# Second layer's modulation weights in rings of their own, loaded two steps ahead, in a two-layer transformer kernel on one NeuronCore

## The chip, the cores and the metric

The kernel runs on 1 core of one Trainium2 chip. The metric is the device time of one execution in microseconds (us). The engines are TensorE (PE for matmuls, PEld for its weight loads), VectorE (DVE), ScalarE (ACT), GpSimd (POOL) and SyncE (SP, which here issues the transfers, DMAs, one after another). TensorE's granted clock is shown as a share of 2.4 GHz; 0.50 is 1.2 GHz.

## The reference

For a sequence of 512 rows of width 1024, each of two layers computes

```python
mod = jnp.einsum('bd,lde->lbe', jax.nn.silu(c), ada_w) + ada_b[:, None]
for i in range(DEPTH):                               # DEPTH = 2
    sh_t, sc_t, g_t, sh_c, sc_c, g_c = [m[:, None] for m in jnp.split(mod[i], 6, axis=-1)]
    h = x * (1.0 + sc_t) + sh_t
    y = mixer_i(h)                                   # layer 0: sparse attention; layer 1: differential attention
    x = _layer_norm(DN_ALPHA * x + (1.0 + g_t) * y, ln_g[i, 0], ln_b[i, 0])
    h = x * (1.0 + sc_c) + sh_c
    y = jnp.square(jax.nn.relu(h @ mlp_w1[i])) @ mlp_w2[i]      # 1024 -> 4096 -> 1024
    x = _layer_norm(DN_ALPHA * x + (1.0 + g_c) * y, ln_g[i, 1], ln_b[i, 1])
```

All is float32. The change concerns `mod` of layer 1: one vector of 1024 times a matrix of 1024 x 6144 (24 MB), which is read from HBM once.

## The kernel before, in words

**Number format.** A float32 product is made of three TensorE passes on rounded parts: each operand x is split into a high part H (a rounded copy, by ACT) and a low part L = x - H (by DVE or POOL). `mm3` and the `step` of `out_proj` issue low x high, high x high, high x low. So each weight piece of 512 KB goes through four places: the load into a tile of ring `raw` (L128, SP; **3 buffers**), the cast to `wh` (L148, ACT), the subtraction to `wl` (L153, POOL and DVE in turn), and the matmuls. `wh` and `wl` have 6 buffers each.

**The MLP** (`mlp`, once for each layer) goes through the hidden width in four quarters q = 0 to 3. In each, the w1 product makes 8 tiles of 128 hidden units x 512 rows (24 matmuls a tile; lines L158 to L160), each followed by `act`: Relu on ACT (L1035), squared on DVE (L1037, tile `ex`, from a PSUM bank into SBUF), split into two pages (L133, L134). Then the w2 product of the quarter, `out_proj` (L549 to L551), has two halves h0 and h1 of 512 output columns: four row tiles i, 8 steps k, 3 matmuls, so 96 matmuls a half. A finished half is evicted by `add_scaled`: four products with the gain on DVE (L459, tile `pt`) and four additions to the residual R on POOL (L460). Banks: six PSUM banks in rings `psd`, `psl`, `pso` of two serve w1 tiles and w2 halves in turn, so a half of w2 can start in a bank only when what was in it has been evicted.

**Side work.** While layer 0's MLP (MLP 0) runs, the generator `side` makes layer 1's modulation: `ada_dve` loads 128 x 1024 weights (512 KB) into ring `raw`, and DVE adds them, scaled by silu(c), to accumulators `vo`: two instructions of 128 x 512 for each load (L429 for the first row block, L431 for the later ones). There are 3 pairs of vectors x 8 row blocks x 2 = 48 such steps. After each pair TensorE sums over the partitions (L436, matmuls with ones), and a copy, transposes and small additions (L439, L405, L415) give the columns `modc`. A `next(side)` stands behind every `act` and every k step of w2 in q = 1 to 3, and three in q = 0. In the same way `affine_later` (L534, L535, POOL) scales and shifts the residual R by the layer norm's pages, 8 steps, one behind each of the first acts of q = 0.

**Order.** The text's order is not the program's: a scheduler with a timeline of its own places the instructions of each engine, and each engine then runs its list in order. A `with tc.issue_after(ins)` keeps DVE instructions of the block behind `ins`; the loads on SP and the matmuls are not bound by it. Waits for data and for free buffers are semaphores. A load waits on SP for its ring's buffer, and every later load on SP waits behind it.

Of the kernel before, what the change touches and what calls it, by code (L numbers as in the profile page):

```python
# [15 lines left out]
ALU = mybir.AluOpType  # L16
# [3 lines left out]
P = 128  # L20
S = 512
D = 1024
DC = D // P
# [44 lines left out]
def hybrid_kernel(  # L68
# [8 lines left out]
    nc = tc.nc  # L77
    x = x[0]
    out = out[0]
# [4 lines left out]
    pg = ctx.enter_context(tc.tile_pool(name="pages", bufs=1))  # L84
# [12 lines left out]
    def page(dt=F32, tag="pg"):  # L97
        return pg.tile([P, 512], dt, tag=tag, name=nm(tag), bufs=GB[tag])
# [3 lines left out]
    def temp(tag, dt=F32):  # L102
        return tp.tile([P, 512], dt, tag=tag, name=nm(tag), bufs=TB[tag])
# [20 lines left out]
    def raw(shape, src, bufs=3):  # L124
        n = shape[0] * shape[1]
        t = wp.tile([P, 1024], F32, tag="raw", name=nm("raw"), bufs=bufs)
        v = t[:, :n].rearrange("p (a b) -> p a b", a=shape[0])
        nc.sync.dma_start(v, src)  # L128
        return v
# [79 lines left out]
    sil = cp.tile([P, 8], F32, name="sil")  # L209
# [29 lines left out]
    adaw = [ada_w[l].rearrange("(k p) n -> p k n", p=P) for l in range(2)]  # L239
# [60 lines left out]
    for kc in range(DC):  # L300
# [9 lines left out]
        a = (hT[0][:, kc, :], hT[1][:, kc, :])  # L310
# [91 lines left out]
    def ada_cols(l, va, vb, res, o, rows=P):  # L402
        ov = o.rearrange("p (m r) -> p m r", m=4)
        for m in range(4):
            nc.tensor.transpose(ov[:, m, 0:rows], res[0:rows, P * m : P * (m + 1)], ident[0:rows, 0:rows])  # L405
        for j in range(rows // 32):
            col = ov[:, :, 32 * j : 32 * j + 1].rearrange("p m o -> p (m o)")
            if vb is not None:
                v, h, partial = (va, vb)[j // 2], j % 2, False
            elif rows < P:  # L410
                v, h, partial = va, j, False
            else:
                v, h, partial = va, j // 2, j % 2 == 1
            c = slice(4 * h, 4 * h + 4)
            nc.vector.tensor_tensor(out=modc[:, l, v, c], in0=col, in1=modc[:, l, v, c] if partial else abcv(l, v)[:, c],  # L415
                                    op=ALU.add)

    def ada_dve(l, va, vb, tag):

        vs = (va,) if vb is None else (va, vb)  # L420
        acc = [page(tag=tag) for _ in range(4 if vb is not None else 2)]
        for k in range(DC):
            for n, v in enumerate(vs):
                r = raw((1, 1024), adaw[l][:, k : k + 1, D * v : D * (v + 1)])
                for h in range(2):
                    src = r[:, 0, 512 * h : 512 * (h + 1)]
                    a = acc[2 * n + h] if vb is not None else acc[h]
                    if k == 0:
                        nc.vector.tensor_scalar(out=a, in0=src, scalar1=sil[:, k : k + 1], scalar2=None, op0=ALU.mult)  # L429
                    else:  # L430
                        nc.vector.scalar_tensor_tensor(out=a, in0=src, scalar=sil[:, k : k + 1], in1=a,  # L431
                                                       op0=ALU.mult, op1=ALU.add)
                yield
        o = bank("t")
        for j in range(4 if vb is not None else 2):
            nc.tensor.matmul(o[32 * j : 32 * j + 32, :], ones[:, 0:32], acc[j], start=True, stop=True,  # L436
                             tile_position=(0, 32 * j))
        n = 128 if vb is not None else 64
        nc.vector.tensor_copy(acc[0][0:n], o[0:n])  # L439
        ada_cols(l, va, vb, acc[0], o, n)  # L440

    def gain(l, v, tag="pg"):

# [148 lines left out]
    def attend(pairs, make, mask, pv, done, out, LA, early=None, depth=1, group=0, side=iter(()),  # L592
# [117 lines left out]
        for _ in ahead:  # L710
# [7 lines left out]
                            op0=ALU.mult)  # L718
# [55 lines left out]
    for i in range(1, NT):  # L774
        W = P * (i + 1)
        acc = page()
        work[i] = acc
        for h in range(IDXH):
# [4 lines left out]
            r = temp("neg")  # L783
# [4 lines left out]
            else:  # L788
                nc.vector.scalar_tensor_tensor(out=acc[:, 0:W], in0=r[:, 0:W], scalar=s, in1=acc[:, 0:W],
                                               op0=ALU.mult, op1=ALU.add)  # L790
# [5 lines left out]
    for i in range(NT):  # L796
        if i % 2 == 0:
            ckb.append(bank("t"))
        o = ckb[-1][:, 256 * (i % 2) : 256 * (i % 2) + 256]
# [195 lines left out]
        return weights(), first, rest  # L995

    def next_mod():
        yield from ada_dve(0, 5, None, "pg")
        n = 0
        for va, vb in ((0, 1), (3, 4), (2, 5)):  # L1000
            for _ in ada_dve(1, va, vb, "vo"):
                n += 1
                if n % 6:
                    yield

    side = next_mod()
    R = [[None, None] for _ in range(NT)]
# [17 lines left out]
    def mlp(l, hT, ln_idx, coef_fn, side):  # L1025
        w1 = mlp_w1[l].rearrange("(k p) n -> p k n", p=P)
        w2 = mlp_w2[l].rearrange("(k p) n -> p k n", p=P)
        nT = []
        aff = affine_later()
        for q in range(4):  # L1030
            aT = []

            def act(o):
                r = temp("neg")
                nc.scalar.activation(r, o, AF.Relu)  # L1035
                a = temp("ex")
                nc.vector.scalar_tensor_tensor(out=a, in0=o, scalar=0.0, in1=r, op0=ALU.max, op1=ALU.mult)  # L1037
                H, L = page(F32R), page(F32R)
                split_sb(a, H, L, nc.vector)
                aT.append((H, L))  # L1040
                next(aff, None)
                if q:
                    next(side, None)

            ws, os = [], []
            for n in range(8):
                c0 = 1024 * q + P * n
                w = wpiece((8, P), w1[:, :, c0 : c0 + P])
                o = wide_bank()
                if q == 0 and n < 4:  # L1050
                    ws.append(w)
                    os.append(o)
                    denseT(o, w, hT, ((0, 256),))
                    if n == 3:
                        for m in range(4):
                            denseT(os[m], ws[m], hT, ((256, 512),))
                            act(os[m])
                else:
                    denseT(o, w, hT)
                    act(o)  # L1060
            if q == 0:
                for _ in aff:
                    pass
                for _ in range(3 if l == 0 else 0):
                    next(side, None)
                gc = gain(l, 5, "vo")
            fin = None
            if q == 3:
                coef = coef_fn() if coef_fn else None
                ln = ln_idx if coef else ln_pages(*ln_idx, "vo")  # L1070

                def fin(i):
                    if coef is not None and not nT:
                        nT.extend(new_hT())
                    finish(R[i], i, ln, coef, nT)

            wo = out_proj(w2[:, 8 * q : 8 * q + 8, :], lambda k: aT[k], 8, (0, 1, 2, 3), (None,) * 4,
                          (None, nc.vector if q == 3 else None))
            for k in range(8):
                next(wo)  # L1080
                if q:
                    next(side, None)
            run_out(wo, R, gc, fin)
        return nT

# [144 lines left out]
```

## Time and profile before

| what | value |
|---|---|
| median of 3 runs | 1328.95 us (1327.79 to 1335.72) |
| the profiled execution | 1328.26 us, its span 1326.5 us |
| PE busy in the span | 1263.0 us, 95% |
| DVE, ACT, POOL busy | 759.9, 503.0, 572.4 us |
| TensorE's granted clock, mean | 0.986 |
| MLP 0 | about 325 to 690 us |
| MLP 1 | about 968 to 1320 us |

"Waits" list, for an engine and a line, the time the engine stood idle just before that line's instructions and the instruction or transfer that ended the wait. A "timeline" lists instructions in order of time, with the idle time before each in brackets. "Windows" cut the span into stretches. L-numbers are lines of the kernel before; behind the change they are some 26 to 30 higher.

### The profile page before, as it was taken

Reading aid. Unit: us, or ns where it says so; the run is one execution under the profiler, and the core shown is the slowest. Engines: PE = TensorE matmul, PEld = TensorE weight load, DVE = VectorE, ACT = ScalarE, POOL = GpSimd, SP = SyncE. Lnnn points to the kernel's source line nnn. Section 1 sums busy time; section 2 is a strip of 40 time slices with the busy share of each in tenths; the row PEclk is TensorE's granted clock in tenths of the full one; section 3 lists DMA queues with packets and bytes.
Section 4 is the critical chain, followed back from the end, with each engine's and each line's share of the span. In section 5 each row is a group of like instructions: output and inputs, shape, how many; then the busy total and the mean of one; then the engine's idle time right before and its main releaser. Section 6 shows DMA issues by size and latency. Waiting matters only on the chain.

```text
span 1326.5 us, 17997 instructions
## 1 busy us (share of the span) xinstructions
PE 1263.0 (95%) x6546; PEld 1018.1 (77%) x6546; DVE 759.9 (57%) x1561; ACT 503.0 (38%) x969; POOL 572.4 (43%) x469
## 2 busy tenths in 40 slices
PE   7999998998998999979999999999899999999997
PEld 4775666677986878857788888877698888888885
DVE  2488769869644655666647276675764242241437
ACT  2454157724431222322424555673353142231320
POOL 1614358506383404505434774451548524424403
PEclk9999999999998999989999999999999999999998
DMA  9828577443525456656522533440044333333311
GB/s 290 222 86 251 147 201 206 123 144 103 176 80 175 159 174 193 188 174 206 159 80 80 159 96 91 137 119 13 23 137 152 100 97 96 96 96 95 95 48 64
DMA packets 170417, 176.82 MB, mean 133 GB/s; under 512 B 12796, under 2 KB 128856, under 8 KB 170328
## 3 DMA queue, kind: packets, MB, share of 16 engines
q1 hardware_dynamic: 170328, 175.67, 45.0%
q8 instruction: 52, 0.85, 0.3%
q14 instruction: 37, 0.30, 0.1%
HBM read 160.93 MB, written 2.12 MB: 123 GB/s over the span
## 4 chain that ended last, share of the span: by engine, by line
PE 51%; DVE 11%; DMA 10%; POOL 4%; issue 2%; ACT 2%; SPq 0%; DVEq 0%; POOLq 0%; ACTq 0%
DMA raw<-in_ada_w_dram 8%; PE psd L158 4%; PE psd L159 4%; PE psd L160 4%; DVE vo L431 2%; DMA raw<-in_mlp_w_dram 2%; PE psl L158 2%; PE psl L159 2%; PE psl L160 2%; PE pso L549 2%; PE pso L551 2%; PE pso L550 2%; PE psl L551 2%; PE psl L550 2%; PE psl L549 2%
## 5 line engine op out<-in xcount | busy, mean ns | idle before, releaser
L153 POOL TENSOR_TENSOR wl<-raw,wh 128x512 fp32r<-128x512 f32 (+1 forms) x226 | 300.8, 1356 | 501.1 <-ACT wh L148 499.3
L148 ACT CAST wh<-raw 128x1024 fp32r<-128x1024 f32 x181 | 189.6, 1049 | 405.2 <-DMA raw<-in_mlp_w_dram 130.7
L153 DVE TENSOR_TENSOR wl<-raw,wh 128x1024 fp32r<-128x1024 f32 x68 | 96.6, 1421 | 121.9 <-ACT wh L148 121.8
L158 PE MATMUL psd<-htl,wh 128*128 128x512 f32 (+1 forms) x400 | 156.8, 392 | 5.0 <-DVE htl L134 4.2
L159 PE MATMUL psd<-hth,wh 128*128 128x512 f32 (+1 forms) x400 | 154.1, 385 | 0.0
L160 PE MATMUL psd<-hth,wl 128*128 128x512 f32 (+1 forms) x400 | 153.6, 384 | 0.0
L460 POOL TENSOR_TENSOR rq<-rq,pt 128x512 f32<-128x512 f32 x66 | 97.9, 1513 | 93.1 <-DVE pt L459 93.0
L431 DVE SCALAR_TENSOR_TENSOR vo<-raw,sil,vo 128x512 f32<-128x512 f32 x84 | 78.7, 976 | 85.9 <-DMA raw<-in_ada_w_dram 85.9
L158 PEld LDWEIGHTS psd<-htl,wh 128*128 128x128 f32 x400 | 76.0, 190 | 27.2 <-DVE htl L134 5.3
L650 ACT ACTIVATE ex<-neg,mx 128x128 f32<-128x128 f32 (+3 forms) x128 | 72.1, 564 | 51.0 <-DVE mx L644 44.8
L134 DVE TENSOR_TENSOR pg<-ex,pg 128x512 fp32r<-128x512 f32 x66 | 66.8, 1013 | 39.4 <-ACT pg L133 39.4
L160 PEld LDWEIGHTS psd<-hth,wl 128*128 128x128 f32 x400 | 75.9, 190 | 15.0 <-POOL bm L637 0.8
L158 PE MATMUL psl<-htl,wh 128*128 128x512 f32 (+1 forms) x224 | 82.1, 366 | 4.2 <-DVE htl L134 4.2
L159 PEld LDWEIGHTS psd<-hth,wh 128*128 128x128 f32 x400 | 76.1, 190 | 12.7
L133 ACT CAST pg<-ex 128x512 fp32r<-128x512 f32 x66 | 40.9, 621 | 117.2 <-DVE ex L1037 116.2
L159 PE MATMUL psl<-hth,wh 128*128 128x512 f32 (+1 forms) x224 | 81.7, 365 | 0.0
L160 PE MATMUL psl<-hth,wl 128*128 128x512 f32 (+1 forms) x224 | 81.3, 364 | 0.0
L549 PE MATMUL psl<-wh,pg 128*128 128x512 f32 x176 | 69.8, 397 | 6.4 <-DVE pt L459 4.8
L549 PE MATMUL pso<-wh,pg 128*128 128x512 f32 x176 | 69.4, 394 | 2.6 <-DVE pt L459 2.6
L549 PE MATMUL psd<-wh,pg 128*128 128x512 f32 x160 | 63.0, 394 | 8.5 <-DVE ex L1037 8.5
L551 PE MATMUL psl<-wh,pg 128*128 128x512 f32 x176 | 69.6, 396 | 0.0
L550 PE MATMUL psl<-wl,pg 128*128 128x512 f32 x176 | 69.5, 395 | 0.0
(309 smaller groups left out, 2952.1 us busy)
## 6 DMA issues: line engine op xcount, KB each, us to landing
raw<-in_mlp_w_dram SPq DMA_DIRECT2D x128, 512.0 KB, 4.1
raw<-in_ada_w_dram SPq DMA_DIRECT2D x80, 512.0 KB, 4.3
raw<-in_b_w_in_dram SPq DMA_DIRECT2D x24, 512.0 KB, 3.8
pg<-pg SPq DMA_DIRECT2D x84, 128.0 KB, 2.5
pg<-in_ada_w_dram SPq DMA_DIRECT2D x32, 256.0 KB, 5.3
raw<-in_a_w_in_dram SPq DMA_DIRECT2D x14, 512.0 KB, 5.1
hk<-tbd SPq DMA_DIRECT2D x16, 256.0 KB, 4.0
raw<-in_a_w_o_dram SPq DMA_DIRECT2D x8, 512.0 KB, 5.4
```

Source lines behind the costliest of these rows:

```text
L134: eng.tensor_tensor(out=L, in0=src, in1=f(H), op=ALU.subtract)
L148: nc.scalar.copy(Hv, r)
L153: eng.tensor_tensor(out=Lv[:, a:b], in0=r[:, a:b], in1=f(Hv[:, a:b]), op=ALU.subtract)
L158: nc.tensor.matmul(o, w[0], a[1], start=first, stop=False)
L159: nc.tensor.matmul(o, w[0], a[0], start=False, stop=False)
L160: nc.tensor.matmul(o, w[1], a[0], start=False, stop=last)
L431: nc.vector.scalar_tensor_tensor(out=a, in0=src, scalar=sil[:, k : k + 1], in1=a, op0=ALU.mult, op1=ALU.add)
L460: eng.tensor_tensor(out=R[h], in0=R[h], in1=t, op=ALU.add)
L549: nc.tensor.matmul(o, al[1], wr[0], start=(k == 0), stop=False)
L550: nc.tensor.matmul(o, al[0], wr[1], start=False, stop=False)
L551: nc.tensor.matmul(o, al[0], wr[0], start=False, stop=(k == nk - 1))
L650: marks["a"] = nc.scalar.activation(e[:, 0:W], neg[:, 0:W], AF.Exp, bias=mx[:, 0:1], scale=-1.0, accum_out=sums[:, m : m + 1]).ins
```

## The change

The part of layer 0 that used the same generator (`ada_dve(0, 5, ...)`) keeps ring `raw`. Layer 1's 48 steps move to `ada_pairs`: each step loads two tiles of 128 x 512 (256 KB each) into rings `hk` and `bm` (3 buffers each, so far used by the attention and the transposed activations), the load of step n + 2 is issued before the adds of step n, and the adds of each side step of q = 1 to 3 stand behind the square of the latest `act` on DVE. `affine_later` makes one step for two acts and one for each k step of w2, and what is left is done behind the w2 steps instead of before the gain.

```diff
--- before.py
+++ after.py
@@ -415,29 +415,55 @@
             nc.vector.tensor_tensor(out=modc[:, l, v, c], in0=col, in1=modc[:, l, v, c] if partial else abcv(l, v)[:, c],
                                     op=ALU.add)
 
-    def ada_dve(l, va, vb, tag):
-
-        vs = (va,) if vb is None else (va, vb)
-        acc = [page(tag=tag) for _ in range(4 if vb is not None else 2)]
+    def ada_dve(l, va, tag):
+
+        acc = [page(tag=tag) for _ in range(2)]
         for k in range(DC):
-            for n, v in enumerate(vs):
-                r = raw((1, 1024), adaw[l][:, k : k + 1, D * v : D * (v + 1)])
-                for h in range(2):
-                    src = r[:, 0, 512 * h : 512 * (h + 1)]
-                    a = acc[2 * n + h] if vb is not None else acc[h]
-                    if k == 0:
-                        nc.vector.tensor_scalar(out=a, in0=src, scalar1=sil[:, k : k + 1], scalar2=None, op0=ALU.mult)
-                    else:
-                        nc.vector.scalar_tensor_tensor(out=a, in0=src, scalar=sil[:, k : k + 1], in1=a,
-                                                       op0=ALU.mult, op1=ALU.add)
-                yield
+            r = raw((1, 1024), adaw[l][:, k : k + 1, D * va : D * (va + 1)])
+            for h in range(2):
+                ada_add(acc[h], r[:, 0, 512 * h : 512 * (h + 1)], k)
+            yield
+        ada_sum(l, va, None, acc)
+
+    def ada_add(a, src, k):
+        if k == 0:
+            nc.vector.tensor_scalar(out=a, in0=src, scalar1=sil[:, k : k + 1], scalar2=None, op0=ALU.mult)
+        else:
+            nc.vector.scalar_tensor_tensor(out=a, in0=src, scalar=sil[:, k : k + 1], in1=a, op0=ALU.mult, op1=ALU.add)
+
+    def ada_sum(l, va, vb, acc):
         o = bank("t")
-        for j in range(4 if vb is not None else 2):
+        for j in range(len(acc)):
             nc.tensor.matmul(o[32 * j : 32 * j + 32, :], ones[:, 0:32], acc[j], start=True, stop=True,
                              tile_position=(0, 32 * j))
-        n = 128 if vb is not None else 64
+        n = 32 * len(acc)
         nc.vector.tensor_copy(acc[0][0:n], o[0:n])
         ada_cols(l, va, vb, acc[0], o, n)
+
+    def ada_pairs(l, pairs, tag):
+
+
+        seq = [(pair, k, v) for pair in pairs for k in range(DC) for v in pair]
+        halves = []
+
+        def load(m):
+            if m < len(seq):
+                _, k, v = seq[m]
+                halves.append([temp(t) for t in ("hk", "bm")])
+                for h, t in enumerate(halves[-1]):
+                    nc.sync.dma_start(t, ada_w[l, P * k : P * (k + 1), D * v + 512 * h : D * v + 512 * (h + 1)])
+
+        load(0), load(1)
+        yield
+        for n, (pair, k, v) in enumerate(seq):
+            load(n + 2)
+            if k == 0 and v == pair[0]:
+                acc = [page(tag=tag) for _ in range(4)]
+            for h, src in enumerate(halves.pop(0)):
+                ada_add(acc[2 * pair.index(v) + h], src, k)
+            if k == DC - 1 and v == pair[1]:
+                ada_sum(l, *pair, acc)
+            yield
 
     def gain(l, v, tag="pg"):
 
@@ -995,13 +1021,10 @@
         return weights(), first, rest
 
     def next_mod():
-        yield from ada_dve(0, 5, None, "pg")
-        n = 0
-        for va, vb in ((0, 1), (3, 4), (2, 5)):
-            for _ in ada_dve(1, va, vb, "vo"):
-                n += 1
-                if n % 6:
-                    yield
+        yield from ada_dve(0, 5, "pg")
+        for n, _ in enumerate(ada_pairs(1, ((0, 1), (3, 4), (2, 5)), "vo")):
+            if n % 6 != 5:
+                yield
 
     side = next_mod()
     R = [[None, None] for _ in range(NT)]
@@ -1029,18 +1052,26 @@
         aff = affine_later()
         for q in range(4):
             aT = []
+            order = {}
+
+            def side_step():
+
+                with tc.issue_after(order["act"]):
+                    next(side, None)
 
             def act(o):
                 r = temp("neg")
                 nc.scalar.activation(r, o, AF.Relu)
                 a = temp("ex")
-                nc.vector.scalar_tensor_tensor(out=a, in0=o, scalar=0.0, in1=r, op0=ALU.max, op1=ALU.mult)
+                order["act"] = nc.vector.scalar_tensor_tensor(out=a, in0=o, scalar=0.0, in1=r, op0=ALU.max,
+                                                              op1=ALU.mult).ins
                 H, L = page(F32R), page(F32R)
                 split_sb(a, H, L, nc.vector)
                 aT.append((H, L))
-                next(aff, None)
+                if len(aT) % 2 == 0:
+                    next(aff, None)
                 if q:
-                    next(side, None)
+                    side_step()
 
             ws, os = [], []
             for n in range(8):
@@ -1059,8 +1090,6 @@
                     denseT(o, w, hT)
                     act(o)
             if q == 0:
-                for _ in aff:
-                    pass
                 for _ in range(3 if l == 0 else 0):
                     next(side, None)
                 gc = gain(l, 5, "vo")
@@ -1078,8 +1107,11 @@
                           (None, nc.vector if q == 3 else None))
             for k in range(8):
                 next(wo)
+                next(aff, None)
                 if q:
-                    next(side, None)
+                    side_step()
+            for _ in aff:
+                pass
             run_out(wo, R, gc, fin)
         return nT
```

How this moves DVE's instructions, at three places. In these rows `ex` is an activation's square, `pg` a part of its split, `wl` a weight's low part, `pt` an eviction of w2, `vo<-raw` or `vo<-hk`, `vo<-bm` an add of the modulation.

**DVE at the end of w2's first half in q = 0.** Before:

```order
L431 SCALAR_TENSOR_TENSOR vo_4247<-raw_4593,sil,vo_4247 128x512
L153 TENSOR_TENSOR wl_4438<-raw_4435,wh_4437 128x1024
L431 SCALAR_TENSOR_TENSOR vo_4248<-raw_4593,sil,vo_4248 128x512
L431 SCALAR_TENSOR_TENSOR vo_4245<-raw_4636,sil,vo_4245 128x512
L431 SCALAR_TENSOR_TENSOR vo_4246<-raw_4636,sil,vo_4246 128x512
L459 TENSOR_TENSOR pt_4403<-psl_4303,vo_4263 128x512
L459 TENSOR_TENSOR pt_4406<-psl_4304,vo_4263 128x512
L459 TENSOR_TENSOR pt_4409<-pso_4305,vo_4263 128x512
L459 TENSOR_TENSOR pt_4412<-pso_4306,vo_4263 128x512
```

Now:

```order
L153 TENSOR_TENSOR wl_4446<-raw_4443,wh_4445 128x1024
L485 TENSOR_TENSOR pt_4411<-psl_4303,vo_4263 128x512
L485 TENSOR_TENSOR pt_4414<-psl_4304,vo_4263 128x512
L485 TENSOR_TENSOR pt_4417<-pso_4305,vo_4263 128x512
L485 TENSOR_TENSOR pt_4420<-pso_4306,vo_4263 128x512
L153 TENSOR_TENSOR wl_4610<-raw_4607,wh_4609 128x1024
L153 TENSOR_TENSOR wl_4707<-raw_4704,wh_4706 128x1024
```

The four evictions stood behind adds of two loads; now no add stands near them.

**DVE at the last activations of q = 2.** Before:

```order
L429 TENSOR_SCALAR vo_5651<-raw_5655,sil 128x512
L429 TENSOR_SCALAR vo_5652<-raw_5655,sil 128x512
L1037 SCALAR_TENSOR_TENSOR ex_5451<-psd_5424,neg_5449 128x512
L134 TENSOR_TENSOR pg_5454<-ex_5451,pg_5453 128x512
L431 SCALAR_TENSOR_TENSOR vo_5651<-raw_5687,sil,vo_5651 128x512
L153 TENSOR_TENSOR wl_5618<-raw_5615,wh_5617 128x1024
L431 SCALAR_TENSOR_TENSOR vo_5652<-raw_5687,sil,vo_5652 128x512
L1037 SCALAR_TENSOR_TENSOR ex_5494<-psd_5467,neg_5492 128x512
L134 TENSOR_TENSOR pg_5497<-ex_5494,pg_5496 128x512
L1037 SCALAR_TENSOR_TENSOR ex_5538<-psl_5511,neg_5536 128x512
```

Now:

```order
L1066 SCALAR_TENSOR_TENSOR ex_5552<-psd_5525,neg_5550 128x512
L432 SCALAR_TENSOR_TENSOR vo_5071<-hk_5467,sil,vo_5071 128x512
L432 SCALAR_TENSOR_TENSOR vo_5072<-bm_5468,sil,vo_5072 128x512
L134 TENSOR_TENSOR pg_5555<-ex_5552,pg_5554 128x512
L1066 SCALAR_TENSOR_TENSOR ex_5598<-psl_5571,neg_5596 128x512
L432 SCALAR_TENSOR_TENSOR vo_5069<-hk_5513,sil,vo_5069 128x512
L432 SCALAR_TENSOR_TENSOR vo_5070<-bm_5514,sil,vo_5070 128x512
L432 SCALAR_TENSOR_TENSOR vo_5071<-hk_5558,sil,vo_5071 128x512
L432 SCALAR_TENSOR_TENSOR vo_5072<-bm_5559,sil,vo_5072 128x512
L134 TENSOR_TENSOR pg_5601<-ex_5598,pg_5600 128x512
L153 TENSOR_TENSOR wl_5881<-raw_5878,wh_5880 128x1024
L1066 SCALAR_TENSOR_TENSOR ex_5649<-psl_5622,neg_5647 128x512
```

Adds on newly loaded `raw` tiles stood between two squares; adds on `hk` and `bm` still do, one or two steps of them behind each square.

**DVE at the end of w2's first half in q = 1.** Before (the last square of q = 1 stands five rows higher):

```order
L431 SCALAR_TENSOR_TENSOR vo_5015<-raw_5053,sil,vo_5015 128x512
L431 SCALAR_TENSOR_TENSOR vo_5016<-raw_5053,sil,vo_5016 128x512
L431 SCALAR_TENSOR_TENSOR vo_5015<-raw_5085,sil,vo_5015 128x512
L431 SCALAR_TENSOR_TENSOR vo_5016<-raw_5085,sil,vo_5016 128x512
L415 TENSOR_TENSOR modc<-pst_4999,abc 128x4 x4
L484 SCALAR_TENSOR_TENSOR nxa_6283<-modc,cols 128x8
L485 SCALAR_TENSOR_TENSOR nxb_6284<-modc,cols 128x8
L486 TENSOR_TENSOR nxb_6284<-nxb_6284,modc 128x8
L153 TENSOR_TENSOR wl_5111<-raw_5108,wh_5110 128x1024
L459 TENSOR_TENSOR pt_5089<-psd_4935,vo_4263 128x512
L459 TENSOR_TENSOR pt_5092<-psd_4936,vo_4263 128x512
L459 TENSOR_TENSOR pt_5095<-psl_4937,vo_4263 128x512
```

Now (the last square stands eighteen rows higher, with adds of seven steps and a half behind it up to here):

```order
L430 TENSOR_SCALAR vo_5071<-hk_5033,sil 128x512
L432 SCALAR_TENSOR_TENSOR vo_5070<-bm_5066,sil,vo_5070 128x512
L430 TENSOR_SCALAR vo_5072<-bm_5034,sil 128x512
L432 SCALAR_TENSOR_TENSOR vo_5071<-hk_5075,sil,vo_5071 128x512
L440 COPY vo_4249<-pst_5039 128x512
L432 SCALAR_TENSOR_TENSOR vo_5072<-bm_5076,sil,vo_5072 128x512
L432 SCALAR_TENSOR_TENSOR vo_5069<-hk_5093,sil,vo_5069 128x512
L485 TENSOR_TENSOR pt_5135<-psd_4963,vo_4263 128x512
L432 SCALAR_TENSOR_TENSOR vo_5070<-bm_5094,sil,vo_5070 128x512
L485 TENSOR_TENSOR pt_5138<-psd_4964,vo_4263 128x512
L485 TENSOR_TENSOR pt_5141<-psl_4965,vo_4263 128x512
L485 TENSOR_TENSOR pt_5144<-psl_4966,vo_4263 128x512
```

The first eviction stood (`pt_5089`) behind adds of three steps; it stands (`pt_5135`) behind the first add of the eleventh step. In q = 2 the evictions stand likewise behind ten steps of adds and the three small instructions that make the next coefficients.

## Rows read from the trace of the kernel before

**Rows 1.** The page, part 1: busy time, share of the span and instructions of each engine.

```profile
PE 1263.0 (95%) x6546; PEld 1018.1 (77%) x6546; DVE 759.9 (57%) x1561; ACT 503.0 (38%) x969; POOL 572.4 (43%) x469
```

**Rows 2.** Windows: busy time and count of each engine, TensorE clock, DMA share, GB/s.

```profile
core 0: us, PE busy (x) PEld busy (x) DVE busy (x) ACT busy (x) POOL busy (x), PEclk, DMA share, GB/s
325.00:401.00 76.00, 75.72 (x430) 66.22 (x430) 43.88 (x49) 30.08 (x44) 46.38 (x32) 0.98 0.44 138
406.00:411.30 5.30, 5.30 (x13) 4.15 (x14) 3.90 (x5) 0.00 (x0) 5.27 (x4) 0.50 0.70 220
411.30:565.90 154.60, 151.31 (x668) 122.98 (x666) 92.30 (x114) 40.04 (x52) 56.04 (x39) 1.00 0.56 177
573.10:578.50 5.40, 5.36 (x16) 2.56 (x17) 2.62 (x4) 2.23 (x4) 0.00 (x0) 0.50 0.53 192
601.00:604.00 3.00, 0.64 (x3) 0.53 (x4) 2.42 (x3) 1.49 (x2) 0.67 (x1) 1.00 0.76 215
968.00:1301.00 333.00, 333.00 (x1560) 279.62 (x1559) 122.50 (x136) 101.83 (x134) 136.66 (x99) 1.00 0.32 97
```

**Rows 3.** Waits of PE from 325 to 690 us: total, times, longest.

```profile
PE psd L549 <- DVE ex L1037: 8.5, 2, 6.9
PE psl L549 <- DVE pt L459: 4.8, 1, 4.8
PE pso L549 <- DVE pt L459: 2.6, 1, 2.6
PE psl L549 <- DVE ex L1037: 1.6, 1, 1.6
```

**Rows 4.** Timeline of DVE: start, duration, instruction, idle before it and releaser.

```profile
403.93 1.41 DVE L431 SCALAR_TENSOR_TENSOR vo<-raw,sil,vo 128x512 f32<-128x512 f32 x2 [4.98 <-DMA raw<-in_ada_w_dram]
...
569.94 0.75 DVE L431 SCALAR_TENSOR_TENSOR vo<-raw,sil,vo 128x512 f32<-128x512 f32 x1 [3.35 <-DMA raw<-in_ada_w_dram]
...
572.41 0.68 DVE L1037 SCALAR_TENSOR_TENSOR ex<-psd,neg 128x512 f32<-128x512 f32 x1
```

**Rows 5.** Waits of DVE from 325 to 690 us.

```profile
DVE vo L431 <- DMA raw<-in_ada_w_dram: 85.9, 33, 15.1
```

**Rows 6.** Timeline of SP, a modulation load's issue.

```profile
333.97 0.34 SPq L128 DMA_DIRECT2D raw<-in_ada_w_dram  x1
```

**Rows 7.** DMA issues from 325 to 690 us: count, KB, median us to landing.

```profile
raw<-in_ada_w_dram SPq DMA_DIRECT2D x48, 512.0 KB, 4.2
pg<-in_ln_b_dram SPq DMA_DIRECT2D x2, 256.0 KB, 6.8
```

**Rows 8.** The page, part 6: DMA issues, count, KB, median us to landing.

```profile
pg<-in_ada_w_dram SPq DMA_DIRECT2D x32, 256.0 KB, 5.3
hk<-tbd SPq DMA_DIRECT2D x16, 256.0 KB, 4.0
```

**Rows 9.** The page, part 5: the adds on DVE.

```profile
L431 DVE SCALAR_TENSOR_TENSOR vo<-raw,sil,vo 128x512 f32<-128x512 f32 x84 | 78.7, 976 | 85.9 <-DMA raw<-in_ada_w_dram 85.9
```

**Rows 10.** Timeline of DVE and then of POOL in the w2 product of q = 0.

```profile
438.36 3.35 DVE L431 SCALAR_TENSOR_TENSOR vo<-raw,sil,vo 128x512 f32<-128x512 f32 x2 [1.31 <-DMA raw<-in_ada_w_dram]
...
423.84 2.54 POOL L153 TENSOR_TENSOR wl<-raw,wh 128x512 fp32r<-128x512 f32 x2 [7.77 <-ACT wh L148]
...
439.41 3.46 POOL L153 TENSOR_TENSOR wl<-raw,wh 128x512 fp32r<-128x512 f32 x2
```

**Rows 11.** Timeline of SP, then DVE, then PE, at MLP 0's start.

```profile
318.25 4.83 SPq L128 DMA_DIRECT2D raw<-in_mlp_w_dram  x2
...
323.22 0.68 DVE L459 TENSOR_TENSOR pt<-psd,hk 128x512 f32<-128x512 f32 x1
...
338.48 0.88 DVE L429 TENSOR_SCALAR vo<-raw,sil 128x512 f32<-128x512 f32 x2 [1.19 <-DMA raw<-in_ada_w_dram]
339.28 0.69 DVE L134 TENSOR_TENSOR htl<-bm,hth 128x512 fp32r<-128x512 f32 x1
...
340.34 0.38 PE L158 MATMUL psd<-htl,wh 128*128 128x256 f32 x1
```

## The prediction

> **What bounds the kernel now.** I read the page's busy times first, then windows over the stages, the waits of PE, the timeline at each wait, and last the queues that load the weights. TensorE is busy 95% of the span [rows 1], so a change to the loads can win only what stands idle or runs at a lowered clock, and only where the changed work runs: MLP 0. MLP 1 is the control: the same products and weights without the side work, and PE busy 333.00 of 333.00 us [rows 2]. MLP 0 stands idle for four waits, 8.5 + 4.8 + 2.6 + 1.6 = 17.5 us [rows 3], all at the borders of the w2 products: it waits for squares (`ex`, L1037) or for evictions (`pt`, L459). Neither is late of itself. The evictions that the 4.8 us waited for stand in DVE's order right behind adds, of which the one at 403.93 (L431) had waited 4.98 us for its load; the square at 572.41, which ends the 6.9 us, follows adds of which the first waited 3.35 us [rows 4]. DVE runs its list in order, so a load that is late for an add is late for everything behind it. In MLP 0 those waits come to 85.9 us [rows 5]; most cost PE nothing, four do.
>
> Two of the waits have a second price. After the one that ends at 406.0 the granted clock is 0.50 (1.2 GHz) over 5.30 us of work, and again over 5.40 us after the 6.9 us wait [rows 2]. Both times PE had stood idle just before. The stretches around show 1.00, so half of this time is lost: 2.65 + 2.7 = 5.35 us. After the wait of about 2.6 us at 601 the next row's clock is not lowered: in 601 to 604 it reads 1.00 [rows 2].
>
> **The change part by part.**
>
> *Layer 1's loads leave `raw`, and adds leave the evictions and squares that were stalled.* In the order of q = 0's end no add stands at the evictions any more, which removes the 4.8 us and its clock stretch. In q = 1 and 2 an add still stands behind each square, but its load is issued two steps ahead into a ring that no weight piece needs, and one or two steps fall to one `act`, that is to 24 matmuls. From [rows 2], 333.00 us / 1560 matmuls = 0.21 us each on the average (some are 256 columns wide; I take 0.22 for a full one), so an `act` comes every 5.3 us. If a step takes less than half of that, no square is held up. Gain if all of it goes: 17.5 + 5.35 = 22.85 us, which makes the profiled execution 1328.26 - 22.85 = **1305.4**.
>
> *What a step takes in a burst.* The adds have no wait ahead of them now except at their own pace p: three buffers, each going round once in issue of two halves, landing, and two adds, so p = (2 x issue + landing + pair of adds) / 3. An issue is 0.34 us [rows 6]. A 256 KB load into these rings isn't in the trace of before. The nearest rows are the same weights, same stage, same queue, at 512 KB: 4.2 us [rows 7]; 256 KB loads elsewhere took 4.0 and 5.3 [rows 8]. A pair of adds took 1.41 us undisturbed [rows 4], 2 x 0.976 = 1.95 on the average [rows 9], and 3.35 beside two subtractions of POOL [rows 10]. Low end: (0.68 + 4.0 + 1.41) / 3 = 2.0. High end: (0.68 + 5.3 + 3.35) / 3 = 3.1. I take (0.68 + 4.2 + 1.95) / 3 = **2.28 us**, from the same stage and the average add.
>
> The Trainium skill speaks against halving the loads ("DMA: Bandwidth & Descriptors", Rules for kernel authors: at least 1 MiB a DMA for bandwidth; Anatomy of one DMA: about 2.0 us fixed for each and 436 GB/s beyond it). By it 256 KB would land in an estimated 2.6 us, and the sum would come out some 2 us lower, since the fixed part is waited for two steps ahead; the traces' 4.0 to 5.3 us agree that half the bytes save little, and not on the size.
>
> *The new piles.* In q = 1 the first eviction of h0 stands behind ten and a half steps since the last square, in q = 2 behind ten. PE has work meanwhile: 96 matmuls of h0 and the first 12 (q = 1) or 14 (q = 2) of h1 in banks that are free, 108 or 110 x 0.22 = 23.8 or 24.2 us; the square comes about 1.5 us after h0 begins, and the ones-matmuls and transposes of the pair's sum give about that back. The pile needs two steps already loaded (2 x 1.95), the rest at p, and the eviction, 0.68 (the same form as the square in [rows 4]); in q = 2 about 1 us of small instructions more. So 4.6 + 8.5p against 23.8, and 5.6 + 8p against 24.2. At p = 2.28 these are 24.0 and 23.8: a tie. I charge 2 us for both. At p = 2.0, nothing. At p = 3.1, 7.2 and 6.2 us, and since waits of that length brought a lowered clock twice, 5.35 more: 18.8 us.
>
> *Start of MLP 0.* The first steps' halves go into `hk`, which holds gain pages until the eviction at 323.22 [rows 11], and they stand on SP ahead of two w1 pieces, the first of which was issued at 318.25. These slip by up to 6 us, POOL's subtraction of one of them now stands ahead of the last row tile's layer norm, and that tile's transposes stand 27 matmuls lower on PE. Of 256 columns these are half of 0.22, so 3 us; PE's first use of that tile at 340.34 came 0.37 us after the last piece was written (339.28 + 0.69). Against it, an add that waited 1.19 us and took 0.88 stood in that chain [rows 11] and doesn't now. 3 - 0.37 - 2.07 = 0.6; bounds 0 and 6 (the whole slip). I take 1.5.
>
> *At nothing.* 48 more issues x 0.34 = 16 us on SP [rows 6], which waits for buffers far longer than it issues. Adds: as many, of the same form. The residual work on POOL keeps its place in POOL's order, and PE was busy 75.72 of 76.00 us while it ran [rows 2]; if it moved, it would have till the evictions of h0. The layer-1 attention's own loads into `hk` wait till the modulation is done, in q = 3, long before they are used. In MLP 1 no side work is left.
>
> Sum: 1305.4 + 1.5 + 2 = 1308.9 for the profiled execution, which lies 0.7 us below the median of before; so **1309.5 us**.
>
> **The rivals.** A difference of 1% (13.3 us, below 1315.7 or above 1342.2) is what a measurement of this kernel can tell from no change.
>
> *Adds that pile up meet POOL.* If nearly every pair takes the 3.35 us of [rows 10], p = (0.68 + 4.2 + 3.35) / 3 = 2.74, the two piles are late by 16.5 x 2.74 - 37.8 = 7.4 us, and with the clock 12.8: 1305.4 + 1.5 + 12.8 + 0.7 = **1320**. For it: POOL's pair of subtractions also lengthened, from 2.54 to 3.46 us, so the two engines do disturb each other. Against it: the average add is 0.976, and POOL was busy 56 of 155 us [rows 2]. Chance 0.13, a third of it short enough to be faster by 1%. The Trainium skill has a rule for this ("SBUF — State Buffer", SBUF: two separate sides): a DVE instruction with two SBUF inputs and a GpSimd one that reads SBUF hold a port pair in turn, and the later is fully blocked. The trace agrees that they collide, but both got longer there.
>
> *Slower: the round trip of the halves sets the pace.* Halves and w2 pieces go out on one queue, each waiting for its buffer in turn. A 256 KB load in this very stage took 6.8 us [rows 7]. With that and disturbed adds p = (0.68 + 6.8 + 3.35) / 3 = 3.61, the piles are late by 21.8 us, and 1305.4 + 1.5 + 21.8 + 5.35 + 0.7 = **1335**. It decides from p = 3.26 (16.5p - 37.8 + 5.35 + 1.5 = 22.85), and makes it slower by 1% from 4.1. For it: DMA shares of 0.5 to 0.7 in these stretches [rows 2]. Against it: that load is of another kind (one row spread to all partitions), and 48 loads of twice the size had a median of 4.2. Chance 0.06, two thirds of it over 1%.
>
> *Nothing comes of it.* If the weights' own way (cast, subtraction, `raw`) is what is late, the same borders wait for it when the adds are gone: about **1328**. Against it: MLP 1 runs that way with no idle time. Chance 0.05.
>
> **How the numbers follow.** The forecast has 0.76; its own range is 1304.5 to 1315.5: from the floor of 1305.4 + 0.7 and 1.5 for the runs' spread, up to the start at its bound of 6 and the piles some 4 us late. The rivals have 0.13, 0.06 and 0.05. Range 1304.5 to 1319: left out are the upper half of the first rival, the other two, and 0.03 below the floor, together 0.2. Faster: 0.76 + 0.04 = 0.80. Within 1%: 0.09 + 0.02 + 0.05 = 0.16. Slower: 0.04.
>
> **What would show it.** Right: in the waits of PE no row of w2 on a square or an eviction over 2 us; the clock 1.00 at the borders of q = 0 and q = 2; DVE's 85.9 us of waits for modulation loads cut to less than half. The halves land in 4 to 5.3 us, and adds in w2 follow each other at 2.0 to 2.6 us a step. Wrong: PE waits in h1 of q = 1 or 2 for an eviction, with adds and their loads ahead of it on DVE (the piles; which rival, the pair's duration and the landing tell); a PE wait of over 3 us for `htl` or a w1 piece near 340 us (the start); waits of DVE or PE on `wl` and `wh` in place of the adds (nothing comes of it).

## The result, and the profile after

| | median | runs | ratio to before |
|---|---|---|---|
| before | 1331.58 us | 4, 1327.79 to 1335.72 | |
| changed | 1314.97 us | 4, 1314.23 to 1315.85 | 0.9882 [0.9861, 0.9903] |

The changed kernel is faster by 1.2%. The forecast was 1309.5 us in a range of 1304.5 to 1319; the time lies 5.5 us above it. The profiled execution took 1314.23 us, 14.0 less than that of before. The waits of PE that were to go are gone, but the gain is smaller than what they were worth. So two things are to be explained: where the gain came from, and what took a part of it back.

The page's busy times and windows of the changed kernel, columns as in [rows 1] and [rows 2]:

```profile
PE 1269.5 (97%) x6546; PEld 1019.1 (78%) x6546; DVE 742.5 (57%) x1561; ACT 505.0 (38%) x969; POOL 571.1 (44%) x469
```

```profile
core 0: us, PE busy (x) PEld busy (x) DVE busy (x) ACT busy (x) POOL busy (x), PEclk, DMA share, GB/s
345.00:690.00 345.00, 345.00 (x1532) 276.17 (x1531) 193.97 (x257) 102.56 (x132) 147.87 (x106) 1.00 0.52 163
954.00:1287.00 333.00, 333.00 (x1560) 279.62 (x1560) 120.92 (x136) 102.21 (x134) 136.03 (x99) 1.00 0.32 97
```

From 345 to 690 us PE has no idle time and a clock of 1.00, as MLP 1 has. But PE's busy time rose by 6.5 us, from 1263.0 [rows 1], for the same 6546 instructions. With the two stretches at 0.50 gone it should have fallen by the 5.35 us that the prediction puts on them, so about 12 us are to be explained: something on PE takes longer, and no wait shows it.

The waits of PE, then of DVE for modulation loads, from 325 to 690 us, and the loads' landing from 320 to 690 us:

```profile
PE psd L158 <- DVE htl L134: 3.0, 2, 2.4
```

```profile
DVE vo L432 <- DMA hk<-in_ada_w_dram: 6.9, 3, 3.5
DVE vo L430 <- DMA bm<-in_ada_w_dram: 1.4, 2, 0.8
DVE vo L432 <- DMA bm<-in_ada_w_dram: 1.0, 2, 0.7
```

```profile
bm<-in_ada_w_dram SPq DMA_DIRECT2D x48, 256.0 KB, 4.8
hk<-in_ada_w_dram SPq DMA_DIRECT2D x45, 256.0 KB, 4.1
```

All four rows of [rows 3] are gone; only the start of MLP 0 waits. DVE's adds at L432 wait 7.9 us for these loads, where the same adds waited 85.9 [rows 5]; the adds of the first row block (L430) wait another 1.4.

The busy time is found in the timeline of PE (columns: start, duration, engine and instruction; a wait before it in brackets), at the four matmuls with ones that sum a pair of vectors. Before the change, the first of the three sums:

```profile
483.37 0.39 PE L551 MATMUL psl<-wh,pg 128*128 128x512 f32 x1
483.69 1.06 PE L436 MATMUL pst<-vo,ones 128*32 128x512 f32 x8
484.69 0.50 PE L549 MATMUL psd<-wh,pg 128*128 128x512 f32 x1
485.02 0.39 PE L550 MATMUL psd<-wl,pg 128*128 128x512 f32 x1
485.25 0.39 PE L551 MATMUL psd<-wh,pg 128*128 128x512 f32 x1
```

And in the changed kernel:

```profile
477.39 0.39 PE L577 MATMUL psd<-wh,pg 128*128 128x512 f32 x1
477.71 1.04 PE L437 MATMUL pst<-vo,ones 128*32 128x512 f32 x2
478.69 0.49 PE L575 MATMUL psd<-wh,pg 128*128 128x512 f32 x1
479.11 1.05 PE L437 MATMUL pst<-vo,ones 128*32 128x512 f32 x2
480.09 0.50 PE L576 MATMUL psd<-wl,pg 128*128 128x512 f32 x1
480.43 0.40 PE L577 MATMUL psd<-wh,pg 128*128 128x512 f32 x1
480.75 1.05 PE L437 MATMUL pst<-vo,ones 128*32 128x512 f32 x2
481.73 0.50 PE L575 MATMUL psl<-wh,pg 128*128 128x512 f32 x1
482.06 0.40 PE L576 MATMUL psl<-wl,pg 128*128 128x512 f32 x1
482.39 1.05 PE L437 MATMUL pst<-vo,ones 128*32 128x512 f32 x2
483.37 0.50 PE L577 MATMUL psl<-wh,pg 128*128 128x512 f32 x1
...
484.17 0.40 PE L577 MATMUL psl<-wh,pg 128*128 128x512 f32 x1
```

All four (x8: each shows as two records) took 1.06 us side by side; each alone takes 1.05. They use 32 columns of the array each (128*32), in four different places (`tile_position`), and side by side they overlap. From 483.37 to 485.25 there are three steps of 0.227 us of w2's own and 1.20 us more. From 477.39 to 484.17 there are nine of w2's own and 6.78 - 9 x 0.227 = 4.74 us more. The difference, 3.54 us, three times, is 10.6 us, most of the 12.

No data held the four matmuls apart in the run. The last add to this pair's accumulators on DVE was

```profile
476.89 0.75 DVE L432 SCALAR_TENSOR_TENSOR vo<-bm,sil,vo 128x512 f32<-128x512 f32 x1 [0.71 <-DMA bm<-in_ada_w_dram]
```

and it ended at 477.64, before the first of the four began at 477.71. The other two sums show the same: the accumulators were complete at 561.19 and 642.53, and the first matmul with ones began at 563.64 and 645.02. What sets them apart is the order in which the scheduler wrote them into PE's list.

### The profile page after: what moved, and what is told of

Read it like the earlier page. It is cut to its first block, busy times and chain, and to the rows that moved or that the text cites. A ratio compares the mean times of both kernels' runs of the same rounds, so it can differ in the third digit from the quotient of the medians.

```text
span 1312.2 us, 18105 instructions
## 1 busy us (share of the span) xinstructions
PE 1269.5 (97%) x6546; PEld 1019.1 (78%) x6546; DVE 742.5 (57%) x1561; ACT 505.0 (38%) x969; POOL 571.1 (44%) x469
## 3 DMA queue, kind: packets, MB, share of 16 engines
HBM read 160.93 MB, written 2.12 MB: 124 GB/s over the span
## 4 chain that ended last, share of the span: by engine, by line
PE 70%; DVE 6%; POOL 2%; issue 1%; DMA 1%; ACT 1%; POOLq 0%; DVEq 0%
PE psd L158 5%; PE psd L159 5%; PE psd L160 5%; PE psl L158 3%; PE psl L159 3%; PE psl L160 3%; PE psl L575 3%; PE psl L577 3%; PE psl L576 3%; PE pso L577 3%; PE pso L575 3%; PE psd L577 3%; PE pso L576 3%; PE pso L158 3%; PE pso L159 3%; PE psd L575 3%
## 5 line engine op out<-in xcount | busy, mean ns | idle before, releaser
L153 DVE TENSOR_TENSOR wl<-raw,wh 128x1024 fp32r<-128x1024 f32 x68 | 92.4, 1359 | 149.9 <-ACT wh L148 149.9
L134 DVE TENSOR_TENSOR pg<-ex,pg 128x512 fp32r<-128x512 f32 x66 | 60.1, 911 | 27.0 <-ACT pg L133 27.0
L575 PE MATMUL pso<-wh,pg 128*128 128x512 f32 x176 | 68.8, 391 | 0.0
L577 PE MATMUL pso<-wh,pg 128*128 128x512 f32 x176 | 68.7, 390 | 0.0
L576 PE MATMUL pso<-wl,pg 128*128 128x512 f32 x176 | 68.7, 390 | 0.0
L158 PE MATMUL pso<-htl,wh 128*128 128x512 f32 (+2 forms) x184 | 68.3, 371 | 0.0
```

Of the source, the lines that this page charges most:

```text
L134: eng.tensor_tensor(out=L, in0=src, in1=f(H), op=ALU.subtract)
L153: eng.tensor_tensor(out=Lv[:, a:b], in0=r[:, a:b], in1=f(Hv[:, a:b]), op=ALU.subtract)
L158: nc.tensor.matmul(o, w[0], a[1], start=first, stop=False)
L575: nc.tensor.matmul(o, al[1], wr[0], start=(k == 0), stop=False)
L576: nc.tensor.matmul(o, al[0], wr[1], start=False, stop=False)
L577: nc.tensor.matmul(o, al[0], wr[0], start=False, stop=(k == nk - 1))
```

## The experiments

All medians below are of 4 runs or more, beside runs of the kernel before on the same chip.

**The ones together.** The accumulators are complete in the order 0, 1 and, a step later, 2, 3; issuing the matmuls from the last to the first makes all of them ready when the first can start. Here `issue_after` names a matmul, so it orders instructions of PE.

```diff
-        for j in range(len(acc)):
-            nc.tensor.matmul(o[32 * j : ...], ones[:, 0:32], acc[j], ...)
+        last = None
+        for j in reversed(range(len(acc))):
+            with tc.issue_after(last) if last is not None else nullcontext():
+                last = nc.tensor.matmul(o[32 * j : ...], ones[:, 0:32], acc[j], ...).ins
```

> The changed kernel, but the four ones-matmuls of a pair's sum are issued from the last accumulator to the first, each behind the one before, so that they stand side by side on PE. Theory A (the change removed all stalls, and gave back 4.74 - 1.20 = 3.54 us for each of three sums because matmuls of 32 columns that overlap when side by side were set apart by w2 matmuls): about 10.6 us below the changed kernel's 1315, so 1304 to 1305. Rival B (the ones cost the same either way, and the missing gain was never there: the stalls' work comes back as busy time): 1314 to 1316. Rival C (as A, but PE now waits for the last accumulator, since nothing of the sum can begin before it): 1306 to 1310, with a wait of PE at the ones line.

Measured: **1305.11 us**, 0.9804 [0.9785, 0.9823], 9.9 below the changed kernel. The first sum in its timeline of PE, and the page's busy times:

```profile
480.28 0.39 PE L579 MATMUL psl<-wh,pg 128*128 128x512 f32 x1
480.60 1.07 PE L439 MATMUL pst<-vo,ones 128*32 128x512 f32 x8
...
482.16 0.39 PE L579 MATMUL psd<-wh,pg 128*128 128x512 f32 x1
```

```profile
PE 1257.5 (97%) x6546; PEld 1016.4 (78%) x6546; DVE 746.6 (57%) x1561; ACT 505.0 (39%) x969; POOL 569.8 (44%) x469
```

Again 1.88 us for three w2 matmuls and the sum. PE's busy time is 12.0 us below the changed kernel's. Theory A holds; B falls. C falls too: PE waited 2.6 us in MLP 0, all of it for `htl` at the start, and nowhere at the sums. This kernel beats both.

**The ones in twos.** The same edit with the order 1, 0, 3, 2.

> The changed kernel, but the ones-matmuls stand in two groups of two. Theory A (a group costs about 1.2 us, whatever is in it, and each sum has 4 groups in the changed kernel, 1 with all together): 2 groups are 2 x 1.2 = 2.4 us a sum, so about 3.6 us above the kernel with all together and 7 us below the changed one: 1308. Rival B (the arrangement costs nothing): 1314 to 1316.

Measured: 1308.98 us (1306.30 to 1311.79), 0.9841 [0.9815, 0.9868]. In the timeline each group of two takes as long as four had:

```profile
478.43 1.05 PE L439 MATMUL pst<-vo,ones 128*32 128x512 f32 x4
...
480.31 1.05 PE L439 MATMUL pst<-vo,ones 128*32 128x512 f32 x4
```

With one, two and four groups a sum: 1305.1, 1309.0, 1315.0 us; by A, from the first, 1308.7 and 1315.7 for the others. The price goes by groups, not by matmuls.

**The ones apart in the kernel before.**

```diff
                              tile_position=(0, 32 * j))
+            if vb is not None and j < 3:
+                yield
```

> The kernel before, with one side step between the four ones-matmuls of a pair's sum, which sets them apart on PE in 3, 3 and 4 groups where there was 1 each. Theory A: 7 more groups at 1.2 us each, about 8 us: 1337 to 1340 where the kernel before takes 1331. Rival B: 1329 to 1333. The side steps fall on other activations too, which may move the stalls by some us either way.

Measured: 1341.16 us, 1.0076 [1.0050, 1.0102], 10 above. The direction is A's, but the run alone doesn't show it: PE's waits for squares and evictions moved (13.0 us in all instead of 17.5), and PE waited 5.8 us for the copy of the sum, which it had not before.

**The residual work undone.**

```diff
-                if len(aT) % 2 == 0:
-                    next(aff, None)
+                next(aff, None)
```

and the rest drained ahead of the gain, as before.

> The changed kernel with the residual work as before the change: one step for each activation, the rest drained ahead of the gain. The prediction charged this part nothing, so 1315 within 1.5 us. Rival: if POOL's residual work early in q = 0 holds up its subtractions of w2's weight pieces, some us more, with PE waiting for wl near 375 to 400 us.

Measured: 1314.37 us, 0.9877 [0.9855, 0.9898], against 1314.97. This part of the change does nothing that can be measured.

**Not queued behind the activation.**

```diff
-                with tc.issue_after(order["act"]):
-                    next(side, None)
+                next(side, None)
```

> The changed kernel without the queueing of side steps behind an activation; own rings, two steps ahead and the residual's spreading stay. The ones-matmuls stand side by side again in PE's order, and adds spread forward into q = 0, ahead of its evictions. Theory A with the own rings as what removed the stalls: 1304 to 1308, that is faster than the changed kernel by the ones. Rival D (the queueing is what removed the stalls, since adds stand ahead of squares and evictions again): the waits of PE for squares or evictions come back, 1315 to 1330.

Measured: 1311.56 us (1308.13 to 1315.57), 0.9855 [0.9825, 0.9885]. Neither theory has it right. The ones stood together, so 10.6 us of the changed kernel's cost were saved, and yet it is 6.5 us slower than the kernel with queue and ones together. Waits of PE from 325 to 690 us, those behind the start:

```profile
PE psl L575 <- DVE pt L485: 0.8, 1, 0.8
PE pso L575 <- DVE ex L1065: 0.8, 1, 0.8
PE psl L575 <- DVE pg L134: 0.3, 1, 0.3
```

The waits for squares, their parts and evictions that come back are 1.9 us. The start costs more. Executions differ in how late they reach MLP 0, so it is counted from a point ahead of all layer-1 modulation loads, the first matmul of layer 0's output projection, to the start of the second half of the first tiles. With queue and ones together, and then without the queue:

```profile
260.30 0.48 PE L983 MATMUL psd<-wh,vo 128*128 128x512 f32 x1
...
341.34 0.39 PE L158 MATMUL psd<-htl,wh 128*128 128x256 f32 x1 [0.26 <-DVE htl L134]
```

```profile
261.60 0.48 PE L981 MATMUL psd<-wh,vo 128*128 128x512 f32 x1
...
345.73 0.38 PE L158 MATMUL psd<-htl,wh 128*128 128x256 f32 x1 [0.93 <-DVE htl L134]
```

That is 81.04 and 84.13 us, so the start costs 3.1. Behind it the clock is 0.57 from 345.70 to 349.40; 15 matmuls 0.213 us apart instead of 0.12 cost about 1.4. Together with the waits that is 6.4 of the 6.8 us by which the two executions differ from the common point to MLP 0's last w2 matmul (435.04 against 428.28). Without the queue, modulation loads and adds move forward: DVE is busy 41.3 us with instructions on `vo` from 320 to 420 us, in the changed kernel 6.1. That they are what delays the start fits and isn't shown by itself.

**Queued, but in the weights' ring.** The kernel before with the queue (and with the ones together, so that they don't count).

```diff
+            def side_step():
+                with tc.issue_after(order["act"]):
+                    next(side, None)
...
                 if q:
-                    next(side, None)
+                    side_step()
```

> The kernel before, with loads of 512 KB in the ring that the weights use, but with the side steps queued behind the latest activation, and with the ones together. Theory G (the own rings removed the stalls): PE still waits for squares, evictions or weights in w2 of MLP 0, 15 us or more in all, with lowered clock after some of the waits: 1320 to 1335. Rival D (the queueing removed them): 1305 to 1310.

Measured: **1371.99 us**, 1.0305 [1.0272, 1.0338], 41 us slower than before and 67 slower than with the own rings. The two largest waits of PE from 325 to 760 us, and the largest of SP (in total, times, longest):

```profile
PE pso L158 <- ACT wh L148: 5.6, 4, 2.5
PE pso L551 <- ACT wh L148: 5.4, 1, 5.4
```

```profile
SPq L128 <- DVE vo L431: 117.6, 40, 19.2
```

An add that is held until an activation holds its `raw` buffer, SP waits for that buffer with weight loads behind it, and PE now waits for weights in w1 as well as in w2. So the queue without own rings loses more than the change wins. The run leaves out the lead of two steps and the halves of 256 KB too, which came with the rings; no run has own rings without any lead, or with loads of 512 KB.

**One step ahead**, ones together.

```diff
-        load(0), load(1)
+        load(0)
...
-            load(n + 2)
+            load(n + 1)
```

> The kernel with the ones together (1305), but each step's halves are issued one step ahead in the text instead of two. Theory E (the lead is what counts): with two steps in flight a step takes (0.68 + 4.4 + 1.95) / 2 = 3.5 us, so the two piles are late by 16.5 x 3.5 - 37.8 = 20 us and lower the clock: 1325 to 1332. Rival F (the ring of three buffers sets the lead, since SP issues a load as soon as a buffer is free): 1304 to 1307.

Measured: 1304.31 us, 0.9805 [0.9780, 0.9831], the same as with two. F holds: in the text the lead is one step less, and the time doesn't show it. That the ring's three buffers set the lead is the reading that fits; the run shows only that the number in the text doesn't.

**Half the ring.** Both halves of a step in `hk`, ones together.

```diff
-                halves.append([temp(t) for t in ("hk", "bm")])
+                halves.append([temp(t) for t in ("hk", "hk")])
```

> The kernel with the ones together (1305), but both halves of a step go through the three buffers of hk, so the ring holds a step and a half instead of three. Theory H (the prediction's account of the piles: a step's pace is the round trip over the steps in flight): p = (0.68 + 4.4 + 1.95) / 1.5 = 4.7 us; in q = 1 the first eviction stands behind seven and a half steps, 1.5 x 1.95 + 6 x 4.7 + 0.68 = 31.8 us against 23.8, 8 us late, in q = 2 about as much, and both lower the clock: about 1326 (1318 to 1340), with PE waiting for evictions at these places. Rival F2 (the scheduler puts so few adds ahead of the evictions that the pace doesn't matter): 1304 to 1309.

Measured: 1313.73 us (1310.82 to 1319.03), 0.9852 [0.9827, 0.9876], 8.6 above the full rings (6.4 by the ratios to the kernel before). Between the two. The profiled execution is the slowest of the four, 1319.03 us. Its timeline of PE, at the common point, at the second half of the first tiles, and at the only two waits behind the start; then DVE's at the pile of q = 1:

```profile
265.11 0.47 PE L983 MATMUL psd<-wh,vo 128*128 128x512 f32 x1
...
348.16 0.38 PE L158 MATMUL psd<-htl,wh 128*128 128x256 f32 x1
...
493.29 1.07 PE L439 MATMUL pst<-vo,ones 128*32 128x512 f32 x8 [2.17 <-DVE vo L432]
...
593.28 0.80 PE L577 MATMUL pso<-wh,pg 128*128 128x512 f32 x1 [2.12 <-DVE pt L487]
```

```profile
473.81 1.40 DVE L432 SCALAR_TENSOR_TENSOR vo<-hk,sil,vo 128x512 f32<-128x512 f32 x2
...
495.83 0.68 DVE L487 TENSOR_TENSOR pt<-psd,vo 128x512 f32<-128x512 f32 x1
```

The piles do become late, at the sum in q = 1 and at an eviction in q = 2, but by 2 us each, not 8. Both waits are followed by a lowered clock, as theory H has it: 0.50 from 494.30 to 497.40 and 0.52 from 593.30 to 596.80, about 1.6 us each. The trace has 14 adds between the last square and the first eviction of q = 1, so seven steps took 495.83 - 473.81 = 22.0 us, where the formula gives 1.5 x 1.95 + 5.5 x 4.7 = 28.8. The formula lets one step's issue, landing and adds follow each other for both halves together; the buffers come free one half at a time, and the next half's load starts while the other's add runs. The start takes 83.05 us from the common point instead of 81.04, 2.0 more. Start, waits and clock come to 9.5 of the 9.9 us by which this execution is longer than that of the full rings from the common point to MLP 0's last w2 matmul (438.15 us). It had reached that point 4.8 us later, with nothing of the change run yet.

## Why the prediction came out as it did

*The waits and their clock, 22.85 us: right.* The floor was 1305.4 us for the profiled execution; with the ones together it was 1304.45. The four waits and both stretches at 0.50 are gone, and nothing came in their place on PE.

*Why they went: half right.* The prediction put it down to own rings and to adds that no longer stand at evictions. The rings with their lead, not queued, keep the waits at 1.9 us; the queue alone makes it 41 us slower. What the queue adds to the rings is the 6.5 us between 1305.1 and 1311.6, of which the profiles show 3.1 at the start, 1.9 in waits and 1.4 in the clock.

*The piles, 2 us: nothing, at the forecast pace.* A pile of ten and a half steps was to take 24.0 us including the eviction. DVE's timeline in q = 1, with the first add behind the last square and the first eviction:

```profile
460.82 1.78 DVE L432 SCALAR_TENSOR_TENSOR vo<-bm,sil,vo 128x512 f32<-128x512 f32 x1
...
466.14 0.74 DVE L432 SCALAR_TENSOR_TENSOR vo<-hk,sil,vo 128x512 f32<-128x512 f32 x1
...
483.25 0.75 DVE L432 SCALAR_TENSOR_TENSOR vo<-hk,sil,vo 128x512 f32<-128x512 f32 x1 [3.48 <-DMA hk<-in_ada_w_dram]
...
489.43 0.68 DVE L485 TENSOR_TENSOR pt<-psd,vo 128x512 f32<-128x512 f32 x1
```

From 466.14 to 490.11, the eviction's end, it took 24.0 us. PE came to that bank at 492.61, 2.5 us later, after a sum that set apart had taken 3.54 longer. With the ones together the tie of the forecast is there:

```profile
466.99 0.74 DVE L432 SCALAR_TENSOR_TENSOR vo<-hk,sil,vo 128x512 f32<-128x512 f32 x1
...
489.37 0.68 DVE L487 TENSOR_TENSOR pt<-psd,vo 128x512 f32<-128x512 f32 x1
...
490.16 0.45 PE L577 MATMUL psd<-wh,pg 128*128 128x512 f32 x1
```

The eviction ends at 490.05 and PE comes at 490.16, so 0.1 us was left. The agreement of the pace is in part luck: the half ring shows the formula to be too long where buffers are few, and here the longest wait for a load, 3.48 us, was made up elsewhere.

*The start, 1.5 us: 0.15.* The second halves began at 340.49 instead of 340.34 [rows 11], 0.3 us later if counted from the common point (259.02 and 259.19). SP's timeline shows why:

```profile
312.88 4.12 SPq L454 DMA_DIRECT2D hk<-in_ada_w_dram  x2
317.83 5.46 SPq L128 DMA_DIRECT2D raw<-in_mlp_w_dram  x3
```

The two halves that stand ahead of the w1 pieces got their buffers before 323.22, the eviction that the prediction named, and the pieces went out at 317.83, not some 6 us after 318.25.

*What failed: "the ones-matmuls and transposes of the pair's sum give about that back".* They have no term of their own in the forecast's sum: they were put at the same cost before and after, that is at nothing, without a reason. The program's order on PE had them side by side before and set apart by one or two w2 matmuls in the change, and the prediction, which counts the ones as PE's work in the piles, didn't follow their order. Three sums of 4.74 us instead of 1.20 are 10.6 us; 1305.4 + 10.6 = 1316.0, and the two terms that came to nothing nearly, 1.5 and 2, had covered a part of it. So it is luck that the time lies in the range: the room above 1309.5 was meant for the start and the piles, which cost almost nothing, and a loss that the prediction didn't see took it. That it is the queue which sets them apart is shown by the kernel without it, where they stand together. Why the scheduler orders them so isn't shown; that its own timeline completes the accumulators one by one behind the queue, and that it places each matmul when its own is ready there, would fit. In the run all were complete before the first began.

*The rivals.* Adds that meet POOL: some do (1.78 us at 460.82), too few for the time to show. The round trip: the halves landed in 4.1 and 4.8 us, not 6.8. "Nothing comes of it" falls with the rings. Halving the loads cost nothing that shows: with the ones together the time is at the floor. The estimate of 2.6 us for 256 KB from the Trainium skill ("DMA: Bandwidth & Descriptors", Anatomy of one DMA) was not met; the page gives that fit for transfers issued from GpSimd, and these go out from SP.

*Nothing for the residual work, SP's 48 issues and MLP 1: right*, by the run with the residual undone, by MLP 1's window, and for the issues by the waits of PE, none of which is on a modulation load.

## What to carry to other kernels

Loads for background work need buffers that the main stream doesn't wait for; in this kernel an order that held back their use without such buffers starved the main stream through the shared ring. When a change reorders one engine's work, look at what that does to the order of each engine that is fed by it: small matmuls that ran together can be placed apart, which no wait shows, only busy time that grew with the same instructions. Releasing them by the last of their inputs kept them together here.

## What the runs showed of the hardware

Four matmuls of 32 columns each, 128x512 float32, side by side in four column places took 1.06 us, two took 1.05 and one took 1.05. Around each group the full-width matmuls lost about 0.2 us: the group began 0.32 us after the matmul before it, where two of w2 stand 0.227 us apart, and the second matmul behind it came 0.33 us after the first. The Trainium skill ("TensorEngine Tiling (Array Packing)", Key Properties) says that tiles work in parallel and that changing the tiling mode drains the engine; the first agrees with 1.06 against 1.05 us, the second with the late starts on both sides of a group. No run here measured the drain by itself.

In MLP 0 of the changed kernel PE had no wait from 345 us on, and its clock stayed at 1.00. Before, the waits of 4.8 and 6.9 us were followed by 0.50, and the wait of 2.6 us was not [rows 2]; with half the ring, waits of 2.17 and 2.12 us were followed by 0.50 and 0.52. So the length of the last wait alone doesn't tell whether the clock falls.
